# Modulation vectors of a two-block model: the products on VectorE, ScalarE and GpSimd, the sum over partitions on TensorE

## The chip, the core and the metric

One core of one Trainium2 chip. The metric is the device time of one execution, in microseconds (us). The engines are TensorE (PE; its weight loads are shown as PEld), VectorE (DVE), ScalarE (ACT), GpSimd (POOL) and SyncE (SP), whose queue issues the loads and stores here.

## The reference

Two blocks work on 512 tokens of width 1024, all in float32. The first has four layers (gated linear attention, GLA; a spatial gating unit, SGU; forgetting attention, FOX; GLA again). The second has two layers, runs on the tokens and on 256 context tokens, and each of its layers also has a feed-forward part (FFN). Every layer begins with a norm whose result is scaled and shifted, and ends with a gated addition to the residual. The shift, scale and gate are the modulation vectors, and only they matter here:

```python
cond = jax.nn.silu(c)
for i in range(DEPTH):
    mod = (cond @ w_mod[i] + b_mod[i])[:, None, :]
    shift, scale, gate = jnp.split(mod, 3, axis=-1)
    h = rms_norm(x, norm_pre_g[i]) * (1.0 + scale) + shift
    ...
    x = x + gate * rms_norm(o, norm_post_g[i])
```

In the first block each layer has 3 vectors of 1024 and one condition. In the second each layer has 6, and two conditions (one for the tokens, one for the context), so that two rows come out of one pass over the weights. A vector is a row of 1024 numbers times a 1024 x 1024 matrix: 4 MB of weights are read for each, and each weight is used once or twice.

## The kernel before

**Projections.** Every large product is done with operands split in two parts: a weight tile of 256 KB ([128, 512] elements) is loaded by SP into a ring of raw buffers (tag `wr`, 5 of them), ACT copies its leading part (line 256, into a ring `wh` of 4) and POOL or DVE subtracts that from the raw tile (line 257, into `wl`, 4 of them). PE then multiplies leading by leading, leading by rest and rest by leading (lines 307 to 309 and 351 to 353). PSUM results are evicted by ACT and DVE. The context stream of the second block has rings of its own (`cwr`, `cwh`, `cwl`).

**Modulation vectors.** The first layer's shift and scale are computed in `setup`, before all else, and are not touched. The other 22 vectors (10 with one condition, 12 with two) come from the generator `mods` (lines 373 to 393). For a vector it takes one PSUM bank, and for each of 8 chunks of 128 rows of the weights it loads [128, 1024] (512 KB, line 382) into one of `WM` = 2 buffers `wm`. One step later it issues four matmuls (line 386): the stationary operand is the condition's chunk, padded to 32 columns, the moving operand 256 columns of the weights, and the four results lie on the four groups of 32 partitions. After 8 chunks DVE evicts the bank (line 390), and SP stores one row per condition in DRAM (line 392). Later `mod_cols` (lines 425 to 438) or `gate_row` reads it back, adds the bias and makes columns or a broadcast row of it. The norm uses the columns on line 502. Line 585 is a gated addition to the residual, line 523 a scaling of a tile in the norm and line 524 the same on ACT.

**Order of the work.** The main stream is a generator, and `drain` takes steps of background queues after each of its steps: 0.6 steps of queue "m" (the vectors, in the order in which they are needed, then a position bias), and a rate by stage of queue "c" (the context stream). Where a vector is needed and not yet put out, `need` puts out all that is left up to it at once:

```python
def step(self, q, n=1):
    self.owed[q] += n
    while self.owed[q] >= 1:
        self.owed[q] -= 1
        if self.bg[q]:
            old, self.sk = self.sk, q
            try:
                next(self.bg[q][0][1])
            except StopIteration:
                self.bg[q].pop(0)
            self.sk = old
```

A vector takes 10 yields of `mods`. The order in which instructions are put out is their priority; a scheduler that simulates the engines' times (`schedule_with_timeline_sim=True`) then fixes the order on each engine and on SP's queue, and on the chip each engine runs its instructions in that order.

## Time and profile before

| | us |
|---|---|
| median of 3 runs | 3319.11 |
| the runs | 3316.0, 3319.11, 3320.16 |
| the profiled execution: span from its first to its last instruction | 3315.4 |

The profile is of one execution. It gives no other time of that execution than its span; the median of the runs lies 3.7 us above it. Line numbers (L386) are those of the kernel before; tiles are named after the stage that made them (`mods.wm` is the buffer `wm` of the stage `mods`; `pa` and `pp` are PSUM banks). "Busy" is the time in which an engine had an instruction running; for PE the ends of overlapping matmuls are modelled. An arrow `<-` after a time names what ended an idle time. A float32 matmul of line 386 appears as two records.

### The profile page before, as it was taken

Reading aid. Unit: us, or ns where it says so; the run is one execution under the profiler, and the core shown is the slowest. Engines: PE = TensorE matmul, PEld = TensorE weight load, DVE = VectorE, ACT = ScalarE, POOL = GpSimd, SP = SyncE. Lnnn points to the kernel's source line nnn. Section 1 sums busy time; section 2 is a strip of 40 time slices with the busy share of each in tenths; the row PEclk is TensorE's granted clock in tenths of the full one; section 3 lists DMA queues with packets and bytes.
Section 4 is the critical chain, followed back from the end, with each engine's and each line's share of the span. In section 5 each row is a group of like instructions: output and inputs, shape, how many; then the busy total and the mean of one; then the engine's idle time right before and its main releaser. Section 6 shows DMA issues by size and latency. Waiting matters only on the chain.

```text
span 3315.4 us, 63038 instructions
## 1 busy us (share of the span) xinstructions
PE 3154.1 (95%) x24399; PEld 2704.3 (82%) x24399; DVE 1699.2 (51%) x3578; ACT 1451.7 (44%) x3189; POOL 1307.3 (39%) x1320
## 2 busy tenths in 40 slices
PE   7999999899999999988989999899999989999999
PEld 4878889778778778887877899889889956789898
DVE  3744564454555555657888667531215476541112
ACT  3434544455444533345545544543325246543323
POOL 2544453322222344443642123554446510154445
PEclk9999999999999999998999999899999979999999
DMA  7355645754436524444753344433333310043332
GB/s 239 87 159 185 194 144 164 234 173 125 147 111 198 162 81 132 153 117 126 188 172 110 86 131 114 155 115 94 117 101 124 102 39 1 25 142 94 98 119 89
DMA packets 487155, 426.36 MB, mean 129 GB/s; under 512 B 108038, under 2 KB 441065, under 8 KB 486857
## 3 DMA queue, kind: packets, MB, share of 16 engines
q1 hardware_dynamic: 486857, 422.35, 42.5%
q8 instruction: 192, 3.15, 0.4%
q14 instruction: 106, 0.87, 0.1%
HBM read 383.66 MB, written 38.03 MB: 127 GB/s over the span
## 4 chain that ended last, share of the span: by engine, by line
PE 75%; DVE 11%; DMA 5%; ACT 4%; issue 3%; POOL 2%; SPq 1%; POOLq 0%; DVEq 0%; ACTq 0%
PE ffn.pp L352 6%; PE ffn.pp L351 6%; PE ffn.pp L353 5%; PE ffn.pp L308 3%; PE ffn.pp L307 3%; PE ffn.pp L309 3%; PE mods.pa L386 3%; PE out.pp L307 2%; PE out.pp L309 2%; PE out.pp L308 2%; DMA mods.wm<-in_w_mod_dram 2%; PE odda.pa L889 1%; PE fox.pp L308 1%; PE fox.pp L309 1%; PE fox.pp L307 1%
## 5 line engine op out<-in xcount | busy, mean ns | idle before, releaser
L257 POOL TENSOR_TENSOR ffn.wl<-ffn.wr,ffn.wh 128x512 fp32r<-128x512 f32 x258 | 333.5, 1294 | 355.0 <-ACT ffn.wh L256 355.0
L256 ACT ACTIVATE ffn.wh<-ffn.wr 128x512 fp32r<-128x512 f32 x258 | 162.5, 631 | 354.9 <-PE ffn.pp L353 144.3
L351 PE MATMUL ffn.pp<-pre.t,ffn.wh 128*128 128x512 f32 x672 | 261.5, 389 | 0.0
L352 PE MATMUL ffn.pp<-pre.t,ffn.wl 128*128 128x512 f32 x672 | 261.5, 389 | 0.0
L353 PE MATMUL ffn.pp<-pre.t,ffn.wh 128*128 128x512 f32 x672 | 261.4, 389 | 0.0
L308 PE MATMUL ffn.pp<-ffn.wl,ffn.t 128*128 128x256 f32 x656 | 185.3, 283 | 0.0
L309 PE MATMUL ffn.pp<-ffn.wh,ffn.t 128*128 128x256 f32 x656 | 184.9, 283 | 0.0
L307 PE MATMUL ffn.pp<-ffn.wh,ffn.t 128*128 128x256 f32 x656 | 184.7, 283 | 0.0
L591 DVE SCALAR_TENSOR_TENSOR ffn.t<-ffn.t,ffn.pp 128x512 f32<-128x512 f32 (+1 forms) x66 | 39.4, 596 | 252.2 <-ACT ffn.t L590 252.1
L257 POOL TENSOR_TENSOR gla.wl<-gla.wr,gla.wh 128x512 fp32r<-128x512 f32 x66 | 87.2, 1321 | 163.7 <-ACT gla.wh L256 158.5
L307 PE MATMUL gla.pp<-gla.wh,pre.t 128*128 128x256 f32 x512 | 149.4, 292 | 0.7 <-ACT gla.t L644 0.4
L308 PE MATMUL gla.pp<-gla.wl,pre.t 128*128 128x256 f32 x512 | 148.8, 291 | 0.0
L309 PE MATMUL gla.pp<-gla.wh,pre.t 128*128 128x256 f32 x512 | 148.4, 291 | 0.0
L353 PEld LDWEIGHTS ffn.pp<-pre.t,ffn.wh 128*128 128x128 f32 x672 | 126.2, 188 | 26.2
L351 PEld LDWEIGHTS ffn.pp<-pre.t,ffn.wh 128*128 128x128 f32 x672 | 126.2, 188 | 26.1
L352 PEld LDWEIGHTS ffn.pp<-pre.t,ffn.wl 128*128 128x128 f32 x672 | 126.2, 188 | 25.8
L257 POOL TENSOR_TENSOR ffn.cwl<-ffn.cwr,ffn.cwh 128x512 fp32r<-128x512 f32 x44 | 60.3, 1370 | 212.4 <-ACT ffn.cwh L256 183.9
L386 PE MATMUL mods.pa<-mods.wm,cond_c 128*32 128x256 f32 x1408 | 121.4, 398 | 16.8 <-DMA mods.wm<-in_w_mod_dram 16.7
L1133 DVE SCALAR_TENSOR_TENSOR ffn.t<-ffn.t,ffn.pp 128x512 f32<-128x512 f32 (+1 forms) x66 | 39.4, 597 | 176.3 <-PE ffn.pp L353 175.7
L256 ACT ACTIVATE ffn.cwh<-ffn.cwr 128x512 fp32r<-128x512 f32 x132 | 82.9, 632 | 102.8 <-PE ffn.pp L353 43.0
L308 PEld LDWEIGHTS ffn.pp<-ffn.wl,ffn.t 128*128 128x128 f32 x656 | 125.9, 192 | 0.2
L307 PEld LDWEIGHTS ffn.pp<-ffn.wh,ffn.t 128*128 128x128 f32 x656 | 125.6, 192 | 0.2
(786 smaller groups left out, 10843.8 us busy)
## 6 DMA issues: line engine op xcount, KB each, us to landing
mods.wm<-in_w_mod_dram SPq DMA_DIRECT2D x176, 512.0 KB
gla.wr<-in_gla_w_in_dram SPq DMA_DIRECT2D x96, 256.0 KB
ffn.wr<-in_w_ffn_gate_dram SPq DMA_DIRECT2D x88, 256.0 KB
ffn.wr<-in_w_ffn_up_dram SPq DMA_DIRECT2D x88, 256.0 KB
ffn.wr<-in_w_ffn_down_dram SPq DMA_DIRECT2D x88, 256.0 KB
fox.wr<-in_fox_w_in_dram SPq DMA_DIRECT2D x64, 256.0 KB
sgu.wr<-in_sgu_w_in_dram SPq DMA_DIRECT2D x48, 256.0 KB
out.res_x<-out.t SPq DMA_DIRECT2D x24, 512.0 KB
```

Source lines behind the costliest of these rows:

```text
L256: nc.scalar.activation(hi, src, AF.Copy)
L257: (lo_eng or nc.vector).tensor_tensor(lo, src, hi.bitcast(F32), op=ALU.subtract)
L307: nc.tensor.matmul(o, H.hi(kk, s), w[0][:, k], start=(kk == 0 and first), stop=False)
L308: nc.tensor.matmul(o, H.hi(kk, s), w[1][:, k], start=False, stop=False)
L309: nc.tensor.matmul(o, H.lo(kk, s), w[0][:, k], start=False, stop=(kk == K - 1 and last))
L351: nc.tensor.matmul(o, wh[:, k], H.hi(kk), start=(kk == 0), stop=False)
L352: nc.tensor.matmul(o, wl[:, k], H.hi(kk), start=False, stop=False)
L353: nc.tensor.matmul(o, wh[:, k], H.lo(kk), start=False, stop=(kk == K - 1))
L386: nc.tensor.matmul(ps[g * 32:(g + 1) * 32, :256], pad[:, j, :], ws[j][:, g * 256:(g + 1) * 256], start=(j == 0), stop=(j == 7))
L591: nc.vector.scalar_tensor_tensor(dst, dst, 1.0, z, ALU.add, ALU.mult)
L889: nc.tensor.transpose(pz[:, j:j + 128], P[:, j0 + j:j0 + j + 128], self.ident)
L1133: nc.vector.scalar_tensor_tensor(f, sg, 0.5, o[1], ALU.mult, ALU.mult)
```

## The change

`mods` works on half vectors of 512 columns. For each half it loads 8 tiles [128, 512] of 256 KB, again with 2 buffers. DVE multiplies the first tile by the first condition, one number per partition, and for the other seven multiplies and adds onto an accumulator. With two conditions, ACT multiplies each tile by the second condition and POOL adds the product onto a second accumulator; there is one buffer for the product. After the 8 chunks PE adds the accumulator's partitions: four matmuls of 128 columns per condition, with a stationary operand of 32 columns of which one is ones and the others zeros. DVE evicts [128, 128], and SP stores 512 columns per condition. Two chunks go into one step; a vector takes 9 yields. The constant `unit` is made in `setup` by three memsets on POOL. The raw weight ring `wr` has 4 buffers and not 5. All comments and docstrings are gone as well.

```diff
@@ setup
         nc.gpsimd.memset(self.zero, 0.0)
+        self.unit = self.const([128, 2, 32], "unit")
+        nc.gpsimd.memset(self.unit, 0.0)
+        for i in range(2):
+            nc.gpsimd.memset(self.unit[:, i, i:i + 1], 1.0)
@@ mods
         pad = self.cond[cname]
-        ps = self.psA()
-        ws = []
-        for k in range(8 + WM - 1):
-            if k < 8:
-                ws.append(self.wp.tile([128, D], F32, name=self.nm("wm"), tag="wm", bufs=WM))
-                nc.sync.dma_start(ws[k], W[k * 128:(k + 1) * 128, v * D:(v + 1) * D])
-            j = k - WM + 1
-            if j >= 0:
+        for c0 in range(v * D, (v + 1) * D, 512):
+            ws = []
+            accs = [self.wp.tile([128, 512], F32, name=self.nm("wacc"), tag=f"wacc{i}", bufs=1) for i in range(ncond)]
+            for k in range(8 + WM - 1):
+                if k < 8:
+                    ws.append(self.wp.tile([128, 512], F32, name=self.nm("wm"), tag="wm", bufs=WM))
+                    nc.sync.dma_start(ws[k], W[k * 128:(k + 1) * 128, c0:c0 + 512])
+                j = k - WM + 1
+                if j >= 0:
+                    c = [pad[:, j, i:i + 1] for i in range(ncond)]
+                    if j == 0:
+                        nc.vector.tensor_scalar(accs[0], ws[j], c[0], None, ALU.mult)
+                    else:
+                        nc.vector.scalar_tensor_tensor(accs[0], ws[j], c[0], accs[0], ALU.mult, ALU.add)
+                    if ncond == 2:
+                        p = self.wp.tile([128, 512], F32, name=self.nm("wprod"), tag="wprod", bufs=1) if j else accs[1]
+                        nc.scalar.activation(p, ws[j], AF.Copy, scale=c[1])
+                        if j:
+                            nc.gpsimd.tensor_tensor(accs[1], accs[1], p, op=ALU.add)
+                if k % 2:
+                    yield
+            ps = self.psA()
+            for i, acc in enumerate(accs):
                 for g in range(4):
-                    nc.tensor.matmul(ps[g * 32:(g + 1) * 32, :256], pad[:, j, :], ws[j][:, g * 256:(g + 1) * 256],
-                                     start=(j == 0), stop=(j == 7))
-            yield
-        sb = self.t("t1", [128, 256])
-        nc.vector.tensor_copy(sb, ps[:, :256])
-        for i in range(ncond):
-            nc.sync.dma_start(scr[i, v * D:(v + 1) * D].rearrange("(g n) -> g n", n=256), sb[i:128:32, :])
+                    nc.tensor.matmul(ps[g * 32:(g + 1) * 32, :128], self.unit[:, i, :], acc[:, g * 128:(g + 1) * 128],
+                                     start=(i == 0), stop=(i == ncond - 1))
+            sb = self.t("t1", [128, 128])
+            nc.vector.tensor_copy(sb, ps[:, :128])
+            for i in range(ncond):
+                nc.sync.dma_start(scr[i, c0:c0 + 512].rearrange("(g n) -> g n", n=128), sb[i:128:32, :])
         yield
@@ constants
-NBUF = {..., 'wr': 5, ...}
+NBUF = {..., 'wr': 4, ...}
```

## Rows read from the trace of the kernel before

**Rows 1.** The page: span, and busy time, share and instructions of each engine.
```profile
span 3315.4 us, 63038 instructions
...
PE 3154.1 (95%) x24399; PEld 2704.3 (82%) x24399; DVE 1699.2 (51%) x3578; ACT 1451.7 (44%) x3189; POOL 1307.3 (39%) x1320
```

**Rows 2.** The page: the chain that ended last, share of the span by engine.
```profile
PE 75%; DVE 11%; DMA 5%; ACT 4%; issue 3%; POOL 2%; SPq 1%; POOLq 0%; DVEq 0%; ACTq 0%
```

**Rows 3.** Windows: length, busy us per engine (instructions), clock, DMA share, GB/s.
```profile
58.00:300.00 242.00, 233.93 (x1679) 195.18 (x1678) 132.80 (x221) 92.31 (x169) 110.54 (x116) 0.99 0.42 129
300.00:1110.00 810.00, 775.71 (x6383) 657.84 (x6382) 428.00 (x927) 389.89 (x879) 264.84 (x262) 0.98 0.56 172
1110.00:1420.00 310.00, 295.62 (x2718) 249.01 (x2717) 179.71 (x363) 123.12 (x261) 130.37 (x158) 0.98 0.43 129
1420.00:3315.00 1895.00, 1812.23 (x13381) 1580.43 (x13379) 940.43 (x2018) 825.11 (x1829) 783.52 (x749) 0.97 0.36 106
```

**Rows 4.** The tile mods.wm: its instructions, what they waited for, who waited.
```profile
L386 PE MATMUL mods.pa<-mods.wm,cond_c x1408: 379/379/637, 58.9 to 1397.0; 128*32 128x256 f32 x176
L382 SPq DMA_DIRECT2D mods.wm<-in_w_mod_dram x176: 327/340/1179, 22.9 to 1391.9; - x176
...
  DMA mods.wm<-in_w_mod_dram: 40.7, 40
...
  PE mods.pa L386: 16.7, 19
```

**Rows 5.** The chain of 58 to 1420 us by line, shares of it.
```profile
by line: PE mods.pa L386 6.2%; DMA mods.wm<-in_w_mod_dram 4.3%; issue 3.4%; PE out.pp L307 3.2%; PE fox.pp L308 3.0%; PE fox.pp L309 3.0%; PE out.pp L308 3.0%; PE fox.pp L307 3.0%; PE out.pp L309 3.0%; PE sgu.pp L307 2.9%; PE sgu.pp L308 2.
```

**Rows 6.** Timeline from 588 us: start, length, engine, line, operation.
```profile
589.06 0.28 PE L351 MATMUL gdnp.pp<-pre.t,gdnp.cwh 128*128 128x256 f32 x1
...
589.27 0.59 PEld L386 LDWEIGHTS mods.pa<-mods.wm,cond_c 128*32 128x32 f32 x16
589.27 1.07 PE L386 MATMUL mods.pa<-mods.wm,cond_c 128*32 128x256 f32 x16
...
590.27 0.39 PE L352 MATMUL gdnp.pp<-pre.t,gdnp.cwl 128*128 128x256 f32 x1
```

**Rows 7.** The windows of rows 3 up to 1420, line 386 alone: sum.
```profile
sum 1362.00, PE 121.39 PEld 31.36; mean PE 40.47 PEld 10.45
```

**Rows 8.** DVE by shape, 58 to 1420 us: busy us, mean ns.
```profile
L257 DVE TENSOR_TENSOR gla.wl<-gla.wr,gla.wh 128x512 fp32r<-128x512 f32 x30 | 27.8, 926 | 37.1 <-ACT gla.wh L256 35.6 <-DMA gdng.t<-gdn_tok_ctx 1.4
...
L585 DVE SCALAR_TENSOR_TENSOR out.t<-out.t,out.rr,out.t 128x512 f32<-128x512 f32 x24 | 19.5, 853 | 2.6 <-POOL out.rr L532 2.4
...
L523 DVE TENSOR_SCALAR pre.t<-out.t,pre.rr 128x512 f32<-128x512 f32 x12 | 6.8, 566 | 6.5 <-POOL pre.rr L532 6.5
...
L257 DVE TENSOR_TENSOR mlap.cwl<-mlap.cwr,mlap.cwh 128x512 fp32r<-128x512 f32 x4 | 2.8, 692 | 10.9 <-ACT mlap.cwh L256 10.9
```

**Rows 9.** ACT by shape, 58 to 1420 us: product by a column.
```profile
L524 ACT ACTIVATE pre.t<-out.t,pre.rr 128x512 f32<-128x512 f32 x12 | 8.6, 719 | 6.5 <-POOL pre.rr L532 6.5
```

**Rows 10.** POOL by line, 58 to 1420 us: two operands, 128x512.
```profile
L257 POOL TENSOR_TENSOR gla.wl<-gla.wr,gla.wh 128x512 fp32r<-128x512 f32 x62 | 82.3, 1328 | 148.4 <-ACT gla.wh L256 145.3 <-issue 2.9
```

**Rows 11.** Waits of SP queue, 58 to 1420: us, times, longest.
```profile
SPq L382 <- PE mods.pa L386: 204.6, 118, 15.1
...
SPq L382 <- DMA mods.wm<-in_w_mod_dram: 41.0, 35, 4.7
```

**Rows 12.** The tile gla.wl: its DVE instructions, ns min/median/max.
```profile
L257 DVE TENSOR_TENSOR gla.wl<-gla.wr,gla.wh x32: 281/693/2737, 43.2 to 1311.8; 128x512 fp32r<-128x512 f32 x31, 128x128 fp32r<-128x128 f32 x1
```

**Rows 13.** The page, costliest groups: weight splits on ACT.
```profile
L256 ACT ACTIVATE ffn.wh<-ffn.wr 128x512 fp32r<-128x512 f32 x258 | 162.5, 631 | 354.9 <-PE ffn.pp L353 144.3
```

**Rows 14.** SP timeline, 588 to 622 us: a vector stored.
```profile
621.57 0.55 SPq L392 DMA_DIRECT2D mod_a<-mods.t  x1
```

**Rows 15.** DVE timeline, 618 to 654 us: its columns ready, used.
```profile
628.81 0.15 DVE L437 SCALAR_TENSOR_TENSOR out.mcol<-out.pa,cols 128x8 f32<-128x8 f32 x1
...
652.66 1.45 DVE L502 TENSOR_SCALAR pre.t<-pre.pa,out.mcol 128x256 f32<-128x256 f32 x3
```

More of the change, by code (lines that the diff above doesn't have):

```diff
@@ L2193, in first_block @@
         self.H = H
-NBUF = {'at': 4, 'sq': 1, 't4': 28, 'wr': 5, 'wh': 4, 'wl': 4, 'cwr': 3, 'cwh': 2, 'cwl': 2, 't2': 10, 't1': 5}
+NBUF = {'at': 4, 'sq': 1, 't4': 28, 'wr': 4, 'wh': 4, 'wl': 4, 'cwr': 3, 'cwh': 2, 'cwl': 2, 't2': 10, 't1': 5}
 WM, WSZ = 2, 512
```

## The prediction

> **What bounds the kernel now.** I read the busy times first. TensorE (PE) is busy 95% of a span of 3315.4 us, VectorE (DVE) 51%, ScalarE (ACT) 44%, GpSimd (POOL) 39% [rows 1]. The median of the three runs shown, 3319.1 us, is 3.7 us above that span; the sum is made against the span, and 3.7 us are added at the end. A difference of 0.2%, 6.6 us, is about what a measurement of this kernel can tell from no change.
>
> Busy is not the same as deciding, so next comes the chain of waits: PE carries 75% of it, DVE 11%, DMA 5%, ACT 4%, POOL 2% [rows 2]. A microsecond taken from PE is thus likely to count, and one added to DVE is likely to be covered.
>
> Then where the changed work runs. The matmuls of the modulation vectors (line 386) start at 58.9 us and the last starts at 1397.0 us [rows 4]; the stretch 58 to 1420 us, 1362 us long, holds all of it. There PE is busy 233.9 + 775.7 + 295.6 = 1305 us (96%), DVE 132.8 + 428.0 + 179.7 = 740.5 us (54%), ACT 605 us (44%), POOL 506 us (37%) [rows 3]. After 1420 us nothing of the change runs except the smaller ring of raw weights. In the chain of this stretch alone, line 386 is the largest single entry with 6.2%, 84 us, and the loads of its operand come second with 4.3%, 59 us [rows 5].
>
> **The change part by part.** There are 22 vectors: 10 with one condition, 12 with two. Before, each takes 8 loads of 512 KB and 8 groups of 4 matmuls over 256 columns, in the trace as 8 records each: 176 groups.
>
> *Removed from PE.* A busy time of overlapping matmuls is no price, so I take a place in the timeline: two groups (16 records) begin at 589.27 us and the next matmul of another line begins at 590.27 us [rows 6], 0.50 us a group. 176 x 0.50 = 88 us; the chain's 84 us agrees and is the lower bound, the busy time of 121 us [rows 7] contains modelled ends of matmuls that overlap. The Trainium skill says the same of such rows (Perfetto Trace Analysis, Identifying the Most-Contended Engine: matmul occupancy is no good measure, because matmuls are pipelined); by busy time the sum would come out 33 us lower than mine. PE also stood 16.7 us waiting for these loads, 19 times [rows 4]; it no longer waits for them. Bounds 0 and the chain's 59 us. I take 17, what PE itself lost.
>
> *Added to PE.* The partitions are added per half vector and condition: 10 x 2 + 12 x 2 x 2 = 68 groups of 8 records over 128 columns. With half the columns, proportion gives 0.25 us; the 16 weight loads of two groups took 0.59 us [rows 6], so 0.30 us a group where they set the pace. I take 0.30: 20 us. Bounds 17 and 34 (no cheaper than before). A new wait stands in PE's order, for the finished sum, 44 times. Before, a group waited 0.095 us on average (16.7/176); the sum passes more engines, so I take twice that, 8 us. Bounds 0 and 44 x 0.88 = 39 us (0.88 us is the mean of the 19 waits). Behind it in PE's order stand the projections' matmuls.
>
> *Added to DVE.* 44 products (tensor_scalar, nearest row 0.566 us) and 308 multiply-adds of 128x512 with all operands in SBUF (nearest row line 585, the same operation, 0.853 us) [rows 8]: 25 + 263 = 288 us. DVE rises from 54% to 75% of the stretch. An added operation matters only where work of the chain stands behind it on DVE. With DVE's 11% of the chain and half an operation of mean delay that is 288 x 0.11 / 2 = 16 us; bounds 0 and 32. The eviction of a vector (line 390) becomes two of half the size: nothing, it lies in DVE's idle time. DVE also takes over the wait for the load, and evictions and weight splits queue behind it. PE and its weight-load queue saw 40.7 us of such waits [rows 4]; twice as many loads make 81 us, and 11% of that is 9 us.
>
> *Added to ACT and POOL.* 12 x 2 x 8 = 192 products on ACT with a scale per partition (0.719 us [rows 9]), 138 us, and 12 x 2 x 7 = 168 adds on POOL (1.328 us [rows 10]), 223 us. By the same reckoning with 4% and 2%: 3 + 2 = 5 us, bounds 0 and 10. Each ACT product after the first waits until POOL has read the only product buffer; ACT's splits of weights stand behind it.
>
> *Loads and SP's queue.* 352 loads of 256 KB in the place of 176 of 512 KB, two in flight, so half the bytes ahead. SP issues one in 0.34 us [rows 4]: 60 us more on SP, and 34 more stores of some 0.5 us [rows 14], 17 us. SP already stands 204.6 + 41.0 us before these loads, waiting for their two buffers [rows 11], with weight loads queued behind; now DVE and ACT free the buffers. I put this at nothing, because ACT's weight split itself waits for PE to free a slot: the weights are there first [rows 13]. If that cover goes, the first rival below is the result.
>
> *One raw weight buffer less* (4 in the place of 5): nothing, by the same row. Upper bound: DMA's 5% of the chain is 166 us, less the 59 of the removed loads; a fifth of the rest is 21 us. The three small memsets at the start run under the first loads.
>
> Sum: -88 - 17 + 20 + 8 + 16 + 9 + 5 = **-47 us**. 3315.4 - 47 + 3.7 = **3272 us**.
>
> **Rivals.** *DVE stands before the loads, and PE runs dry (slower).* Before, a step issued one load and used the one of a step earlier. Now a step issues two and uses one of them at once: 22 x 2 x 4 = 176 operations on DVE ask for a load issued just before. If each holds DVE for the 0.88 us that a wait took, that is 155 us; with half reaching PE, 77 us, the 77 us that PE gains net (88 + 17 - 20 - 8) are gone, and the 21 us for the other engines remain: 3340 us. It decides from 0.44 us a load reaching PE. For it: the vectors of a layer's head come shortly before the norm that uses them; one is stored at 621.57 us, its columns are ready at 628.81 us and used at 652.66 us [rows 14, 15], only 24 us of slack. Against it: 1362 - 740 - 288 = 334 us of idle DVE, and weights that are ahead. Chance 0.12.
>
> *DVE and POOL hold each other up, and the gain is eaten.* The same subtraction takes 0.692 us on average in one stage and 0.926 us in the GLA projections [rows 8], with a longest case of 2.737 us [rows 12]. That is what two engines on one port would look like. With 0.926 us for the new operations (22 us more) and 0.234 us for a foreign DVE operation at each of the 168 adds (39 us), DVE gets 349 us. If a fifth of it reaches the end, 70 us in the place of my 16 + 9, the time is 3317 us: no change. Against it: even then DVE is at 80% of the stretch, under PE. The Trainium skill has this as a rule that speaks against the change (GPSIMD Engine Reference, Specifications: GpSimd's SBUF interfaces are shared with VectorE, with contention from VectorE instructions with two SBUF inputs, which the multiply-add is). By that rule, the trace agrees in kind; chance 0.10.
>
> *All of the chain's share goes.* If the loads' 59 us go and not 17, the sum is -84 - 59 + 20 + 30 = -93 us: 3226 us. For it: the chain of the stretch. Against it: a chain names one path, and the next is usually close. Chance 0.18.
>
> *It does nothing.* The matmuls may only have filled gaps that the slow chains of the GLA layer leave on PE; then the 88 us turn into idle time: about 3319 us. Against it: line 386 on the chain. Chance 0.05.
>
> **How the numbers follow.** The forecast, 3272 us, has 0.55. Faster by over 0.2%: 0.55 + 0.18 + 0.02 of the second rival = 0.75. Within 0.2%: 0.05 of the second and 0.03 of the last = 0.08. Slower: 0.12 + 0.03 + 0.02 = 0.17. The range goes from 3215 us, just under the third rival, to 3330 us, past "no change" with the 21 us of the buffer bound largely spent. Some 0.07 lie below and 0.10 above.
>
> **What would show it.** Right: 544 matmul records on the new line, under 30 us; PE busy in 58 to 1420 us (and what takes its place) down by some 70 us; DVE near 1030 us and still under PE in that stretch; the time after 1420 us unchanged within a few us. Wrong: PE idle time in that stretch grown by over 50 us with DVE or wl as the releaser (first rival), multiply-adds of over 0.93 us (second), or waits for raw weights after 1420 us (the buffer).

## The result and the profile after

The changed kernel takes 3479.9 us (median of 4 runs, 3471.6 to 3486.2) where the kernel before took 3319.1 us beside it (4 runs, 3316.0 to 3320.2): slower by a ratio of 1.049, 95% interval 1.0465 to 1.0514, that is by 161 us. The forecast was 3272 us, faster, and its range ended at 3330. One run of the experiments is left out below, the first of the edit e9: it took 3685.7 us at a granted clock of 0.78 in its last 1895 us, where the two kernels' profiles and every other profile here show 0.96 to 0.98.

The page of the changed kernel: its span, the busy time of each engine, and the three groups that took over the products (L396 the multiply-add, L400 the ScalarE product, L402 the GpSimd addition).

```profile
span 3475.0 us, 62851 instructions
...
PE 3141.8 (90%) x23535; PEld 2744.6 (79%) x23535; DVE 2057.1 (59%) x3952; ACT 1567.1 (45%) x3380; POOL 1587.5 (46%) x1491
...
L396 DVE SCALAR_TENSOR_TENSOR mods.wacc<-mods.wm,cond_c,mods.wacc 128x512 f32<-128x512 f32 x308 | 304.4, 988 | 137.2 <-DMA mods.wm<-in_w_mod_dram 135.3
...
L402 POOL TENSOR_TENSOR mods.wacc<-mods.wacc,mods.wprod 128x512 f32<-128x512 f32 x168 | 242.9, 1446 | 159.9 <-ACT mods.wprod L400 121.4
...
L400 ACT ACTIVATE mods.wprod<-mods.wm,cond_c 128x512 f32<-128x512 f32 x168 | 121.1, 721 | 157.9 <-DMA mods.wm<-in_w_mod_dram 81.1
```

The span grew by 159.6 us against [rows 1] and TensorE's busy time shrank by only 12.3. DVE got 358 us more, ACT 115, POOL 280. The multiply-add takes 988 ns on average, where I had 853; the addition 1446, where I had 1328; the product 721 against 719.

Where the time went is told by the windows, cut 1895 us before the end as in [rows 3]; the vectors' last matmul starts at 1492.6 us. These are the columns of [rows 3]: length, busy us of PE, PEld, DVE, ACT and POOL, granted clock, DMA share, GB/s.

```profile
58.00:300.00 242.00, 219.17 (x1427) 193.68 (x1426) 182.54 (x284) 96.19 (x177) 126.88 (x120) 0.93 0.41 120
300.00:1110.00 810.00, 673.01 (x5139) 602.17 (x5140) 582.34 (x1020) 402.44 (x851) 388.00 (x318) 0.89 0.50 151
1110.00:1580.00 470.00, 402.14 (x3420) 349.82 (x3417) 335.56 (x595) 224.86 (x480) 272.72 (x268) 0.91 0.43 126
1580.00:3475.00 1895.00, 1812.64 (x13330) 1578.65 (x13328) 934.86 (x2006) 823.52 (x1825) 781.91 (x748) 0.97 0.36 105
```

The last 1895 us stand beside the last 1895 us of before [rows 3]: PE busy 1812.64 us and 1812.23 us, the same. So nearly all of the loss lies in the stretch of the vectors, 58 to 1580 us in the place of 58 to 1420 us (a later projection, `oddq`, starts its first matmul at 2757.5 us and 2606.5 us before, so 151 of the 160 us are lost by then). PE is busy 1294 us in the stretch (1305 before) and idle 228 us (57 before), and its granted clock is 0.89 to 0.93 where it was 0.98 to 0.99.

The same stretch in one piece, first whole, then the vectors' new matmul line (L408) alone:

```profile
58.00:1580.00 1522.00, 1294.31 (x9980) 1145.67 (x9979) 1100.44 (x1898) 723.50 (x1507) 787.61 (x705) 0.90 0.47 138
58.00:1580.00 1522.00, 30.27 (x544) 12.67 (x544) 0.90 0.47 138
```

The vectors' own matmuls fell from 121.39 us [rows 7] to 30.27, but PE as a whole is busy only 11 us less. By the difference all other matmuls of the stretch are busy 80 us longer. Of that, 67 more of their records in the stretch make some 9 us; the other 70 us are slower matmuls, at a granted clock of 0.90 in the place of 0.98. So the loss has two parts, 171 us more idle time on PE and 80 us of longer busy time, against 91 us that the vectors' line gave back.

What PE waits for is the third view. First its longest waits in 58 to 1580 us of the changed kernel (us, times, longest), then two lines of the kernel before, 58 to 1420 us.

```profile
PE pre.pa L515 <- DVE pre.t L544: 53.1, 7, 12.1
PE fox.pa L1068 <- DVE fox.t L966: 16.1, 6, 4.2
PE glah.pa L744 <- POOL glah.t L737: 11.2, 16, 2.5
PE glah.pa L744 <- DVE glah.t L738: 9.9, 10, 1.7
PE fox.pa L910 <- ACT fox.at L885: 9.7, 5, 3.6
...
PE mods.pa L408 <- POOL mods.wacc L402: 7.4, 4, 2.6
```

```profile
PE glah.pa L723 <- POOL glah.t L716: 8.9, 16, 1.2
...
PE pre.pa L494 <- DVE pre.t L523: 0.8, 2, 0.4
```

The largest wait is for `pre.t` of the norm at a layer's head: 53.1 us, where the same wait took 0.8 us before. The others are chains of small DVE, ACT and POOL operations in GLA and FOX, a few microseconds each. PE's wait for the vectors' own sums is small, 7.4 us for the one from POOL. No single wait makes 171 us of new idle time; many late results of other work add up to it.

Last, the tile `mods.wm` and SP's queue, which answer to [rows 4] and [rows 11].

```profile
L389 SPq DMA_DIRECT2D mods.wm<-in_w_mod_dram x352: 322/335/1751, 22.9 to 1479.7; - x176
L396 DVE SCALAR_TENSOR_TENSOR mods.wacc<-mods.wm,cond_c,mods.wacc x308: 716/752/2904, 34.4 to 1485.0; 128x512 f32<-128x512 f32 x154
...
  DVE mods.wacc L396: 135.3, 117
  ACT mods.wprod L400: 81.1, 34
```

```profile
SPq L389 <- DVE mods.wacc L396: 207.1, 177, 4.1
...
SPq L389 <- ACT mods.wprod L400: 66.8, 58, 4.0
SPq L389 <- DMA mods.wm<-in_w_mod_dram: 55.6, 60, 2.9
```

DVE stands 135.3 us in 117 waits before its loads, and SP 330 us for the two buffers (246 us before). That looks like the first rival. The experiments speak against it.

One seam shows the pattern: the head of the second layer, 352 to 381 us. The windows (columns as above) and the PE timeline of the changed kernel (start, length, engine, line, operation, idle before and its releaser):

```profile
352.00:370.00 18.00, 5.26 (x30) 3.42 (x30) 13.86 (x24) 7.46 (x21) 10.73 (x14) 0.50 0.44 135
370.00:381.00 11.00, 7.20 (x31) 6.53 (x32) 9.89 (x18) 7.06 (x17) 8.03 (x12) 0.50 0.58 200
```

```profile
361.68 0.65 PE L408 MATMUL mods.pa<-mods.wacc,unit 128*32 128x128 f32 x8 [2.47 <-POOL mods.wacc L402]
370.60 1.94 PE L515 MATMUL pre.pa<-ident,pre.t 128*128 128x128 f32 x8 [8.27 <-DVE pre.t L544]
...
378.84 0.41 PE L312 MATMUL sgu.pp<-sgu.wh,pre.t 128*128 128x256 f32 x1
379.05 0.41 PE L313 MATMUL sgu.pp<-sgu.wl,pre.t 128*128 128x256 f32 x1
...
381.28 0.28 PE L313 MATMUL sgu.pp<-sgu.wl,pre.t 128*128 128x256 f32 x1
381.39 0.28 PE L314 MATMUL sgu.pp<-sgu.wh,pre.t 128*128 128x256 f32 x1
```

DVE's timeline in the same stretch:

```profile
346.36 2.42 DVE L606 SCALAR_TENSOR_TENSOR out.t<-out.t,out.rr,out.t 128x512 f32<-128x512 f32 x2
348.70 2.41 DVE L396 SCALAR_TENSOR_TENSOR mods.wacc<-mods.wm,cond_c,mods.wacc 128x512 f32<-128x512 f32 x2
351.85 1.48 DVE L544 TENSOR_SCALAR pre.t<-out.t,pre.rr 128x512 f32<-128x512 f32 x1 [0.73 <-POOL pre.rr L553]
...
360.87 1.03 DVE L394 TENSOR_SCALAR mods.wacc<-mods.wm,cond_c 128x512 f32<-128x512 f32 x1 [1.07 <-DMA mods.wm<-in_w_mod_dram]
363.02 0.75 DVE L396 SCALAR_TENSOR_TENSOR mods.wacc<-mods.wm,cond_c,mods.wacc 128x512 f32<-128x512 f32 x1 [1.11 <-DMA mods.wm<-in_w_mod_dram]
...
369.96 0.48 DVE L544 TENSOR_SCALAR pre.t<-out.t,pre.rr 128x512 f32<-128x512 f32 x1 [0.47 <-POOL pre.rr L553]
```

PE is busy 5.26 of 18 us, and one idle time of 8.27 us ends when DVE delivers `pre.t`. Meanwhile DVE works through residual additions (L606), the norm's scaling (L544, which makes `pre.t`) and the vectors' multiply-adds by turns; it stands 1.07 us before a load at 360.87 and 1.11 us at 363.02, and single operations are stretched: L544 takes 1.48 us at 351.85, where POOL has an addition of the vectors running (from 351.78 us, 1.27 us long), and 0.48 us at 369.96, where POOL has only operations of one column. The granted clock of the stretch is 0.50, the lower of the two levels (in the kernel before it is 1.00 from 320 to 360 us, where the same layer begins): the matmuls of 128x256 start 0.21 us apart up to 379.05 us, and 0.11 us apart at 381.28.

### The profile page after: what moved, and what is told of

Same layout as the page of the kernel before. It is cut to its first block, busy times and chain, and to the rows that moved or that the text cites. A ratio compares the mean times of both kernels' runs of the same rounds, so it can differ in the third digit from the quotient of the medians.

```text
span 3475.0 us, 62851 instructions
## 1 busy us (share of the span) xinstructions
PE 3141.8 (90%) x23535; PEld 2744.6 (79%) x23535; DVE 2057.1 (59%) x3952; ACT 1567.1 (45%) x3380; POOL 1587.5 (46%) x1491
## 5 line engine op out<-in xcount | busy, mean ns | idle before, releaser
L262 POOL TENSOR_TENSOR ffn.wl<-ffn.wr,ffn.wh 128x512 fp32r<-128x512 f32 x258 | 333.6, 1294 | 356.5 <-ACT ffn.wh L261 355.7
L396 DVE SCALAR_TENSOR_TENSOR mods.wacc<-mods.wm,cond_c,mods.wacc 128x512 f32<-128x512 f32 x308 | 304.4, 988 | 137.2 <-DMA mods.wm<-in_w_mod_dram 135.3
L402 POOL TENSOR_TENSOR mods.wacc<-mods.wacc,mods.wprod 128x512 f32<-128x512 f32 x168 | 242.9, 1446 | 159.9 <-ACT mods.wprod L400 121.4
L400 ACT ACTIVATE mods.wprod<-mods.wm,cond_c 128x512 f32<-128x512 f32 x168 | 121.1, 721 | 157.9 <-DMA mods.wm<-in_w_mod_dram 81.1
L314 PE MATMUL gla.pp<-gla.wh,pre.t 128*128 128x256 f32 x512 | 153.2, 300 | 3.3 <-DVE pre.t L262 3.3
L312 PE MATMUL gla.pp<-gla.wh,pre.t 128*128 128x256 f32 x512 | 153.5, 300 | 2.8 <-ACT gla.t L665 2.4
```

Of the source, the lines that this page charges most:

```text
L262: (lo_eng or nc.vector).tensor_tensor(lo, src, hi.bitcast(F32), op=ALU.subtract)
L312: nc.tensor.matmul(o, H.hi(kk, s), w[0][:, k], start=(kk == 0 and first), stop=False)
L314: nc.tensor.matmul(o, H.lo(kk, s), w[0][:, k], start=False, stop=(kk == K - 1 and last))
L396: nc.vector.scalar_tensor_tensor(accs[0], ws[j], c[0], accs[0], ALU.mult, ALU.add)
L400: nc.scalar.activation(p, ws[j], AF.Copy, scale=c[1])
L402: nc.gpsimd.tensor_tensor(accs[1], accs[1], p, op=ALU.add)
```

## The experiments

Three explanations are told apart here. **Loads:** DVE, ACT and SP stand before the loads of the vectors (the first rival). **Work:** the operations added to DVE, ACT and POOL delay other work in their order, whatever they wait for. **Shape:** half tiles, with half the bytes ahead, cost by themselves. Times stand against the kernel before in the same round (3318 to 3323 us) or against the changed kernel's 3480 us, whose four runs lie 15 us apart.

**e1: the multiply-adds on 16 columns.**

```diff
-nc.vector.scalar_tensor_tensor(accs[0], ws[j], c[0], accs[0], ALU.mult, ALU.add)
+nc.vector.scalar_tensor_tensor(accs[0][:, :16], ws[j][:, :16], c[0], accs[0][:, :16], ALU.mult, ALU.add)
```

> The changed kernel, but the 308 multiply-adds on VectorE take 16 of the 512 columns (the first vector of each pair of conditions is therefore left out of the computation but for 16 columns of each half). Every wait for a load stays, the work goes. Theory 'waits' (VectorE stands in order before the half loads, 135 us of waiting in the changed kernel): hardly better, 3430 to 3480 us. Theory 'work' (the 304 us of multiply-adds delay what stands behind them on VectorE): most of the 160 us comes back, 3300 to 3360 us.

3428.5 us (one run), 51 less than the changed kernel. DVE's waits for the loads did not go but rose to 211.5 us (135.3 before). DVE's work counts, and its standing there costs less than it looks. The cut operations still take 133 us on DVE, so 172 us of work were taken away.

**e2: the multiply-adds read no load.** Their work stays; the sum is not that of the weights.

```diff
-nc.vector.scalar_tensor_tensor(accs[0], ws[j], c[0], accs[0], ALU.mult, ALU.add)
+nc.vector.scalar_tensor_tensor(accs[0], accs[0], c[0], accs[0], ALU.mult, ALU.add)
```

> The changed kernel, but the multiply-adds read the accumulator twice and not the loaded tile (the first condition's vectors are left out of the computation). The work stays at 512 columns, VectorE no longer waits for loads, and SP's loads no longer wait for VectorE. Theory 'waits': most of the 160 us comes back, 3300 to 3370 us. Theory 'work': 3420 to 3480 us.

3484.0 us (one run): 4 us above the changed kernel. The multiply-adds themselves got 19 us longer in total (1051 ns each), so the 135.3 us that DVE stood before loads can be worth some 15 us at most. ACT still stands 81.8 us before its loads here, so the run says nothing of ACT's waits.

**e3: the second condition left out.** No products on ACT, no additions on POOL; the context's rows are not computed.

```diff
-            accs = [self.wp.tile([128, 512], F32, name=self.nm("wacc"), tag=f"wacc{i}", bufs=1) for i in range(ncond)]
+            accs = [self.wp.tile([128, 512], F32, name=self.nm("wacc"), tag=f"wacc{0}", bufs=1)] * ncond
...
-                    if ncond == 2:
+                    if False:
```

> The changed kernel with the second condition left out: no products on ScalarE, no adds on GpSimd, 24 multiplies and 168 products and adds fewer, the first condition's sum is stored in both rows. VectorE does all that it did. Theory 'second condition' (GpSimd's adds hold VectorE up and ScalarE waits for the one product buffer): most of the 160 us comes back, under 3360 us. Theories 'waits' and 'work' of VectorE alone: 3400 to 3470 us.

3383.4 us (one run): 96 of the 161 us come back. DVE waits for the loads as it did (133.5 us), and its multiply-adds take 870 ns in the place of 988.

**e4 to e6, e8 and e15: the shape of the loads.** e4 is the kernel before with TensorE's products on the half tiles and steps of the changed kernel:

```diff
+for c0 in range(v * D, (v + 1) * D, 512):
...
-                ws.append(self.wp.tile([128, D], F32, name=self.nm("wm"), tag="wm", bufs=WM))
+                    ws.append(self.wp.tile([128, 512], F32, name=self.nm("wm"), tag="wm", bufs=WM))
...
-                    nc.tensor.matmul(ps[g * 32:(g + 1) * 32, :256], pad[:, j, :], ws[j][:, g * 256:(g + 1) * 256],
+                        nc.tensor.matmul(ps[g * 32:(g + 1) * 32, :128], pad[:, j, :], ws[j][:, g * 128:(g + 1) * 128],
...
+                if k % 2:
+                    yield
```

> The kernel before, products still on TensorE, but on half tiles of 256 KB with two buffers and two loads a step as in the changed kernel (5 raw weight buffers as before). Theory 'smaller loads' (half the bytes ahead, twice the issues, SP's queue blocked): a good part of the 160 us appears here too, 3380 us or more. Theories 'waits' or 'work' on VectorE: within 20 us of before plus some 30 us for the doubled number of matmuls, 3310 to 3360 us.

3404.6 us (one run), 83 more than the kernel before. PE waits 36.7 us for the loads in the place of 16.7, and SP stands 406 us before them. e5 is e4 with four half tiles in flight, so as many bytes ahead as before:

```diff
-WM, WSZ = 2, 512
+WM, WSZ = 4, 512
```

> The kernel before on half tiles of 256 KB, two loads a step, but with four buffers and a use three loads later: the same bytes in flight as before. Theory 'too little in flight' (two half buffers make each load wait for the one before the last, SP's queue stands there, and weights and residual loads behind it come late): most of the 83 us that the half tiles cost with two buffers comes back, 3310 to 3345 us. Theory 'twice the loads and matmuls' (number of issues, fixed cost of small matmuls): stays at 3380 us or more.

3373.4 us, ratio 1.0159 (1.0129 to 1.0189) to the kernel before: 53 us more, outside the 3310 to 3345 that I gave to bytes in flight as the whole cause. Some 30 of the 83 come back. (With four buffers a vector takes 11 steps and not 9, so e5 and e6 also spread the vectors over more of the order.) e15 is e4 with a `yield` after every load and 1.14 steps in the place of 0.6:

```diff
-                if k % 2:
-                    yield
+                yield
...
-MRATE, MB = 0.6, 2
+MRATE, MB = 1.14, 2
```

> The kernel before on half tiles, two buffers, but one load in each step as before and 1.14 steps in the place of 0.6, so that the vectors keep their pace. Two loads in one step: the loss falls from 83 to under 40 us, 3360 us or less. Half tiles themselves (half the bytes ahead, 17 us more matmul): 3385 us or more.

3412.4 us, ratio 1.0273 (1.0242 to 1.0303): as slow as e4. Two loads in one step are not what costs; the half tiles are, in part through the bytes ahead (e5). e8 is the kernel before with every 512 KB load issued as two of 256 KB into the same buffer:

```diff
-nc.sync.dma_start(ws[k], W[k * 128:(k + 1) * 128, v * D:(v + 1) * D])
+for h in range(2):
+    nc.sync.dma_start(ws[k][:, h * 512:(h + 1) * 512], W[k * 128:(k + 1) * 128, v * D + h * 512:v * D + (h + 1) * 512])
```

> The kernel before with each 512 KB load of the vectors' weights issued as two of 256 KB into the two halves of the same buffer. Theory 'too little in flight': within 15 us of before, since as many bytes are ahead. Theory 'twice the loads': 3350 us or more.

3334.4 us (one run; before 3311.3 to 3330.3 in seven): 11 us over the median of before and 4 us over its longest run, so the 176 extra issues cost little, and one run can't tell how little. e6 gives the changed kernel four half tiles in flight, paid for with raw buffers:

```diff
-NBUF = {..., 'wr': 4, ...}
-WM, WSZ = 2, 512
+NBUF = {..., 'wr': 2, ...}
+WM, WSZ = 4, 512
```

> The changed kernel with four buffers of 256 KB and a use three loads later; the room comes from the raw weight ring, 2 in the place of 4. Theory 'too little in flight': 3400 to 3440 us (40 to 80 us better than the changed kernel's 3480), if the two raw buffers cost nothing; the stretch after the vectors, where only the raw ring differs, shows their price by itself. Theory 'work on VectorE and GpSimd': within 25 us of 3480 us in the stretch of the vectors.

3500.0 us (one run), 20 more than the changed kernel, though DVE's waits for the loads fell from 135.3 us to 31.3 and ACT's from 81.1 to 11.5. Two raw buffers fewer are in that number, and their price is not known (one fewer cost 13 us, e13 below), so it says no more than this: with the waits nearly gone nothing was gained that two raw buffers don't eat up. Together with e2 it leaves little room for the theory of the loads where DVE is concerned; for ACT it rests on e6 alone.

**e9: all added operations on 16 columns** (the first product of a half vector keeps its 512). It is the shape of the changed kernel without most of its work.

```diff
... (the multiply-adds as in e1)
-nc.scalar.activation(p, ws[j], AF.Copy, scale=c[1])
+nc.scalar.activation(*((p[:, :16], ws[j][:, :16]) if j else (p, ws[j])), AF.Copy, scale=c[1])
...
-nc.gpsimd.tensor_tensor(accs[1], accs[1], p, op=ALU.add)
+nc.gpsimd.tensor_tensor(accs[1][:, :16], accs[1][:, :16], p[:, :16], op=ALU.add)
```

> The changed kernel with the multiply-adds, the products (all but the first of a half vector) and the additions cut to 16 columns; loads, waits, steps and matmuls as they are. The sums are left out but for 16 columns. Work in the engines' order (my theory): almost all of the loss goes, 3290 to 3370 us, and the norm's matmuls wait less than 30 us for pre.t. The loads' pattern (two half tiles in a step, one used at once, the rival): the loss stays for the most part, 3400 us or more.

3358.6 us (two runs), ratio 1.0122 (1.0069 to 1.0176) to the kernel before. 121 of the 161 us go with the work, though DVE's wait for the loads rises to 214 us. But PE still waits 51.6 us for `pre.t` over the whole span, more than the 30 I had said, and 41 us of loss remain: the shape, the smaller ring and what PE gives up are together no gain. The cut operations still take time (106 us the multiply-adds, 51 the products, 51 the additions), so not all of the 41 is the shape. In the stretch of the vectors alone the wait for `pre.t` is still this:

```profile
PE pre.pa L515 <- DVE pre.t L544: 32.2, 10, 5.2
```

So more than half of the longest wait of the list, 53.1 us, stays without most of the added work.

**e13, e10, e14, e16, e11: the work alone, beside TensorE's products.** These leave the kernel before as it is, with its 512 KB loads, and put the changed kernel's operations beside the matmuls; nobody reads what they compute. All have 4 raw buffers, to make room, so e13, which is that alone, is their zero. They ran in two rounds, so the differences are taken between the ratios; each of them is good to some 10 us either way.

```diff
-NBUF = {..., 'wr': 5, ...}
+NBUF = {..., 'wr': 4, ...}
```

> The kernel before with 4 raw weight buffers in the place of 5, nothing else. If the buffer costs nothing, as the last 1895 us of the two kernels say: 3310 to 3330 us. If the runs that add work to the kernel before owe part of their loss to it: 3335 us or more, and that much is to be taken off each of them.

3335.2 us (10 runs), ratio 1.0040 (1.0024 to 1.0056): 13 us, and not nothing. e10 adds DVE's work:

```diff
+acc = self.wp.tile([128, 512], F32, name=self.nm("wacc"), tag="wacc0", bufs=1)
...
+for h in range(2):
+    wj = ws[j][:, h * 512:(h + 1) * 512]
+    if j == 0 and h == 0:
+        nc.vector.tensor_scalar(acc, wj, pad[:, j, 0:1], None, ALU.mult)
+    else:
+        nc.vector.scalar_tensor_tensor(acc, wj, pad[:, j, 0:1], acc, ALU.mult, ALU.add)
```

> The kernel before (raw ring 4), with the changed kernel's work on VectorE put beside TensorE's: one product and 15 multiply-adds of 128x512 for each vector, on the two halves of each 512 KB tile; nobody reads their sum. TensorE's work, the loads' size and their steps stay as before. Work in the order: about the 51 us that cutting these operations took off the changed kernel, 3350 to 3400 us, with PE's wait for pre.t up from 18.7 to 35 us or more. Loads' pattern: within 10 us of the kernel before.

3404.8 us, ratio 1.0251 (1.0217 to 1.0285). Less e13's 0.40% that is 2.1%, 70 us. PE's wait for `pre.t` did not rise as I had said (20.9 us over the span, 18.7 before). That wait in the vectors' stretch, DVE's new group there, and the window that answers to [rows 3] (the profiled run, 3386.0 us, is the shortest of the four):

```profile
PE pre.pa L501 <- DVE pre.t L530: 2.6, 3, 1.0
```

```profile
L394 DVE SCALAR_TENSOR_TENSOR mods.wacc<-mods.wm,cond_c,mods.wacc 128x512 f32<-128x512 f32 x327 | 280.7, 858 | 154.0 <-DMA mods.wm<-in_w_mod_dram 150.5
```

```profile
58.00:1489.00 1431.00, 1337.57 (x10724) 1120.40 (x10723) 999.06 (x1847) 601.58 (x1301) 539.32 (x534) 0.96 0.48 145
```

PE has the same work, 10724 matmuls against the 1679 + 6383 + 2718 of [rows 3], and is idle 93 us in the place of 57 and busy 1338 us in the place of 1305, at a clock of 0.96 in the place of 0.98. Half of the loss of that run is idle time in small pieces, half is slower matmuls. e14 is e10 without the reads of the weights:

```diff
-nc.vector.scalar_tensor_tensor(acc, wj, pad[:, j, 0:1], acc, ALU.mult, ALU.add)
+nc.vector.scalar_tensor_tensor(acc, acc, pad[:, j, 0:1], acc, ALU.mult, ALU.add)
```

> As the kernel before with VectorE's added work, but the 330 multiply-adds read their own sum twice and no weights; only the first operation of a vector reads a tile. Their time on VectorE stays, its wait for the loads (150.5 us, 75 times) and its share in setting the buffers free go. The work itself: 3380 to 3410 us, as with the waits. The waits: 3340 us or less.

3416.0 us, ratio 1.0275 (1.0244 to 1.0307), 78 us over e13. The waits for the loads make none of e10's loss: it is the operations. e16 adds only the second condition's products on ACT:

```diff
+for h in range(2 if ncond == 2 else 0):
+    p = self.wp.tile([128, 512], F32, name=self.nm("wprod"), tag="wprod", bufs=1)
+    nc.scalar.activation(p, ws[j][:, h * 512:(h + 1) * 512], AF.Copy, scale=pad[:, j, 1:2])
```

> The kernel before (raw ring 4) with the 192 products of 128x512 on ScalarE alone, without GpSimd's additions; nobody reads them. If GpSimd's additions make the loss (VectorE stretched beside them, ScalarE held by the product buffer): within 25 us of e13. If ScalarE's own 138 us make it: 3370 us or more.

3362.6 us, ratio 1.0117 (1.0083 to 1.0151): 0.77% or 26 us over e13, for 192 products of 0.72 us. ACT also stands 93.8 us before the loads in this run, and no run here takes that away from it by itself, so the 26 us are the products and their waits together:

```profile
L390 ACT ACTIVATE mods.wprod<-mods.wm,cond_c 128x512 f32<-128x512 f32 x192 | 138.0, 719 | 94.9 <-DMA mods.wm<-in_w_mod_dram 93.8
```

e11 adds POOL's additions too:

```diff
     nc.scalar.activation(p, ws[j][:, h * 512:(h + 1) * 512], AF.Copy, scale=pad[:, j, 1:2])
+    if j:
+        nc.gpsimd.tensor_tensor(p, p, p, op=ALU.add)
```

> The kernel before (raw ring 4), with the second condition's work put beside TensorE's: for each vector with two conditions 16 products on ScalarE and 14 additions on GpSimd, 128x512 each, through one buffer; nobody reads them. Work in the order: towards the 96 us that leaving the second condition out took off the changed kernel, 3370 to 3430 us. If VectorE's work alone counts: within 15 us of the kernel before.

3388.4 us, ratio 1.0217 (1.0195 to 1.0238), another 1.0% or 33 us for the additions and for ACT's wait for the one product buffer (47.0 us):

```profile
L392 POOL TENSOR_TENSOR mods.wprod<-mods.wprod 128x512 f32<-128x512 f32 x168 | 183.0, 1090 | 152.0 <-ACT mods.wprod L390 141.5
L390 ACT ACTIVATE mods.wprod<-mods.wm,cond_c 128x512 f32<-128x512 f32 x192 | 138.1, 719 | 92.5 <-POOL mods.wprod L392 47.0
```

The additions take 1090 ns here, where they read one buffer twice, and 1446 ns in the changed kernel, so e11 has 183 us of the 243 us of POOL's work. One line tells what POOL does to DVE: the gated addition to the residual (line 585 of the kernel before, 853 ns there [rows 8]), in e16 and then in e11, by shape, 58 us to the vectors' end:

```profile
L588 DVE SCALAR_TENSOR_TENSOR out.t<-out.t,out.rr,out.t 128x512 f32<-128x512 f32 x24 | 19.9, 869 | 4.4 <-POOL out.rr L535 4.2
```

```profile
L590 DVE SCALAR_TENSOR_TENSOR out.t<-out.t,out.rr,out.t 128x512 f32<-128x512 f32 x24 | 27.6, 1190 | 3.1 <-POOL out.rr L537 1.6 <-DMA gla.wr<-in_gla_w_in_dram 1.2
```

The same 24 operations take 869 ns beside ACT's products and 1190 ns when POOL's additions run too. By the Trainium skill (SBUF — State Buffer, on the port pair that DVE and GpSimd share) a DVE instruction with two SBUF inputs contends with a GpSimd instruction that reads SBUF; the trace agrees, 321 ns an operation here. It is not the whole picture: the norm's scaling (L523 of the kernel before), which has one tensor as input, rises too, from 581 to 780 ns, and DVE's subtractions of weights, which have two, by 65 ns at most.

**e12: a mixture.** DVE's method for the ten vectors with one condition, out of 512 KB loads that hold two row chunks of a half vector; TensorE's for the other twelve.

```diff
+if ncond == 1:
+    yield from self.mods1(scr, cname, W, v)
+    return
...
+ws.append(self.wp.tile([128, 2, 512], F32, name=self.nm("wm"), tag="wm", bufs=WM))
+nc.sync.dma_start(ws[k], W[k * 256:(k + 1) * 256, c0:c0 + 512].rearrange("(a p) n -> p a n", p=128))
...
```

> The ten vectors with one condition by VectorE's multiply-adds, out of 512 KB loads that hold two row chunks of a half vector, one load in a step as before; the twelve with two conditions by TensorE as before. Raw ring 4. TensorE loses 80 groups of 0.50 us and gets 20 of 0.30 us, 34 us less. Work in the order: VectorE's 140 us cost at the rate of 51 for 288 some 25 us: 3310 us, within 20 either way. If only the pattern of the loads cost time: 3285 us.

3349.5 us, ratio 1.0090 (1.0068 to 1.0112): 17 us over e13's level by the ratios, outside what I gave it. So 140 us of DVE work and the changed loads cost more than 34 us less on TensorE gave. That raised the next question.

**e17 and e18: TensorE's work taken away, nothing added.** Parts of the columns are left out of the sums. In e17 seven of a vector's eight chunks have one matmul in the place of four:

```diff
-for g in range(4):
+for g in range(4 if j == 0 else 1):
...
-                                     start=(j == 0), stop=(j == 7))
+                                     start=(j == 0), stop=(j == (0 if g else 7)))
```

> The kernel before with 11 of the 32 matmuls of a vector: the first chunk has all four, the other seven only one each (their other three quarters of the columns are left out of the sums). Loads, waits, buffers, steps as before; nothing is added. 21/32 of 88 us, 58 us, go if a matmul taken from TensorE counts in full as the prediction had it: 3262 us (3250 to 3275). If half of it only turns into idle time on TensorE: 3290 us. If all of it: 3320 us.

e17 took 3345.0 us, ratio 1.0079 (1.0052 to 1.0106), and its expectation was built on a wrong price. PE's timeline, one group of four matmuls (8 records) in the kernel before and one group of one (2 records) in e17:

```profile
618.07 0.64 PE L386 MATMUL mods.pa<-mods.wm,cond_c 128*32 128x256 f32 x8
618.64 0.38 PE L308 MATMUL out.pp<-out.wl,sgu.t 128*128 128x256 f32 x1
```

```profile
621.64 0.62 PE L386 MATMUL mods.pa<-mods.wm,cond_c 128*32 128x256 f32 x2
622.19 0.38 PE L309 MATMUL out.pp<-out.wh,sgu.t 128*128 128x256 f32 x1
```

0.57 us for four, 0.55 us for one: the four go to four groups of 32 columns of the array and run side by side, as the Trainium skill describes it (TensorE: Matmul & The Clock Gate, Packing small matmuls). e17 thus took next to nothing from PE (the line is busy 112 us in the place of 121). That it still lost 26 us says what an edit of this kernel can cost in itself; like e13's, it may put all instructions after it in another order. The 26 us of e16, the 33 of e11 and the 17 of e12, each taken by itself, are of that size; the 70 and 78 of DVE's operations and the 59 of e11 over e13 are well above it.

e18 is e17 with the one matmul of the middle six chunks cut to 16 columns, which does take time from PE:

```diff
... (the loop over g and the stop flag as in e17)
-nc.tensor.matmul(ps[g * 32:(g + 1) * 32, :256], pad[:, j, :], ws[j][:, g * 256:(g + 1) * 256],
+n = 256 if j in (0, 7) else 16
+nc.tensor.matmul(ps[g * 32:(g + 1) * 32, :n], pad[:, j, :], ws[j][:, g * 256:g * 256 + n],
```

> The kernel before, where of a vector's eight chunks the middle six have one matmul of 16 columns each in the place of four of 256 (the rest is left out of the sums), the first has all four and the last one of 256. Loads, waits, buffers and steps as before; nothing is added. Six of eight groups, 132, fall from 0.50 us to about 0.15: 46 us less on TensorE. If that counts in full: 3274 us, or some 3295 with the 15 to 26 us that small edits of this kernel have cost (e8, e13, e17). If it turns into idle time: 3320 to 3345 us.

PE's timeline in e18, two groups:

```profile
320.96 0.30 PE L387 MATMUL mods.pa<-mods.wm,cond_c 128*32 128x16 f32 x4
321.19 0.39 PE L307 MATMUL out.pp<-out.at,gla.t 128*128 128x256 f32 x1
```

0.23 us, so 0.115 us a group in the place of 0.50. The windows of e18 up to the vectors' end and after it, then the first of them for the vectors' line alone (sum):

```profile
58.00:1420.00 1362.00, 1271.64 (x9867) 1116.63 (x9865) 740.20 (x1512) 606.17 (x1310) 509.03 (x536) 0.95 0.51 154
1420.00:3315.00 1895.00, 1804.80 (x13372) 1574.53 (x13370) 937.15 (x2018) 823.91 (x1828) 787.14 (x749) 0.97 0.37 106
```

```profile
sum 1362.00, PE 60.43 PEld 25.91; mean PE 60.43 PEld 25.91
```

The line's own busy time fell from 121.39 us [rows 7] to 60.43. PE as a whole is busy 33.6 us less in the stretch than before [rows 3]: by the difference the other matmuls got 27 us longer, at a clock of 0.95 in the place of 0.98, and the rest became idle time, 90 us in the place of 57. The time is 3325.0 us (12 runs), ratio 1.0011 (0.9995 to 1.0026): nothing gained over the kernel before. But e17 is the same edit with PE's time left in, and over e17 the gain is 0.68% or some 23 us of the 57 us (132 groups from 0.55 to 0.115 us) that were taken. So between none and two fifths of a microsecond taken from PE reached the end, by which of the two is the zero; in full it did not count by either.

## Why the prediction was wrong

**Point by point,** by the terms of the sum. Shares are in us of 3320; e2 and e4 are single runs:

| term | predicted | measured | by |
|---|---|---|---|
| matmuls taken from PE, with their waits | -88 - 17 | for 132 of 176 groups: 0, or -23 | e18 against before, or against e17 |
| the other matmuls of the stretch | 0, not named | some +70 us of busy time, clock 0.90 for 0.98 | changed kernel |
| one group of 128 columns on PE | 0.30 us | 0.29 us (two from 673.20 to 673.78 us) | changed kernel |
| DVE's operations | +16 | +70, +78 | e10, e14 less e13 |
| DVE's waits for the loads | +9 | nothing | e2, e14 |
| ACT's products | +3 | +26, with ACT's waits for loads | e16 less e13 |
| POOL's additions | +2 | +33, with ACT's waits for the buffer | e11 less e16 |
| loads and SP's queue | 0 | with PE as the consumer +83; the shape with little work +41, buffer included | e4; e9 |
| one raw buffer less | 0, bound 21 | +13 | e13 |

The shape with little work (41) and the three kinds of work (70 + 26 + 33) make 170 us, where 161 were measured. That is near, but no proof that the parts are complete: e9 still has part of the work in its 41, each part is good to 10 us or so, and taken away from the changed kernel the work is worth 51 us (e1) and 96 (e3) in two parts, but 121 at once (e9).

**The step that failed first** is the cover of the added operations: "an added operation matters only where work of the chain stands behind it on DVE", priced by an engine's share of the chain times half an operation. DVE's operations reach the end with a quarter of their time (70 of some 290 us), ACT's and POOL's with a fifth (26 of 138; 33 of 183); I had 6, 2 and 1%. An engine's share of the chain tells what a given order waits for. In the changed kernel PE's new waits lie in the norms, in GLA and in FOX, where DVE, ACT, POOL and PE take turns on small tiles: idle time of 46% on DVE was not idle time at those places, where DVE was the engine that PE waited for (53.1 + 16.1 + 9.9 us in the list above). That the added operations alone make these waits is not shown: of the 53.1 us for `pre.t`, 32.2 stay when the work is cut to 16 columns (e9), and DVE's work beside the old matmuls makes 2.6 (e10).

The sum also has no term for what idle time does to the clock. It took PE's other matmuls to stay as long as they were, and they got some 70 us longer (0.90 in the place of 0.98).

**The second** is the -88 us. "A microsecond taken from PE is thus likely to count" was read from PE's 75% of the chain. The price of a group was right in the timeline, and taking it away for 132 groups left the end where it was: the time became idle time and slower matmuls. That is the fourth rival, to which I gave 0.05. What e18 can't tell is whether a gain of 13 to 26 us is hidden under what small edits cost here; against e17 it is 23.

**The cover of the loads**, put at nothing, is the third. The row that I took for it [rows 13] is of the FFN, whose first split runs at 2126.5 us, after the last vector; it says nothing of the stretch where the loads changed. There half tiles cost 83 us with PE as the consumer (e4).

**The first rival** had the sign and not the mechanism. DVE does stand before the loads, 135.3 us, as it said. But without those waits nothing is gained (e2, e14), nor with four loads in flight and two raw buffers fewer (e6). The signature that I had written down for it, PE idle time grown by over 50 us with DVE as the releaser, came true, and would have misled: the releaser is DVE for the norm's `pre.t` and not for the sums. **The second rival** had a mechanism that is there: multiply-adds at 988 ns, over the 0.93 us that I had set as its sign, against 870 ns in e3 and 858 in e10 without POOL's additions; and L590 above. Its 70 us for DVE is near what e10 and e14 measured, by a fifth of 349 us where the runs have a quarter of 290; what it had wrong is that it left PE's gain and the small prices of ACT, POOL and the loads in place. **The third rival** left the 8 us of PE's new wait out of its sum, which would be 3234 us with them.

**What held:** PE's matmuls on the new line are 544 records and busy 30.3 us, just over the 30 I had said; the product on ACT 0.721 us; the time after the vectors unchanged. **What didn't:** PE busy in the stretch fell by 11 us and not by 70, and DVE rose to 1100 us and not 1030, though still under PE. Of the raw buffer's 13 us, 7 lie in the vectors' stretch (their last matmul starts at 1404.2 us in e13 and at 1397.0 before), and not only after 1420 us, where I had looked for them.

**What stays open.** Which order of instructions makes the loss is not shown: the kernel's scheduler lays out every engine's order anew for each edit, and the waits that grew are many and small (in e10's stretch none but that for the vectors' own loads is over 9.0 us). Why half tiles cost 83 us where PE reads them is settled only in part: 30 us come back with as many bytes ahead (e5), some 17 are longer matmuls (by an estimate, 352 groups of 0.30 us against 176 of 0.50), the rest is not told apart. Nor is it told apart how much of ACT's 26 us is its waits for loads, and why most of the wait for `pre.t` stays in e9. None of the versions was faster than the kernel before.

## What to carry to other kernels

A high share of the busy time, or of the chain of waits, doesn't show that an engine's time counts in full, nor that its neighbours are covered: before work is moved from it to "idle" engines, take some of it away, and put the same work on the others with nobody reading it. Both are edits of a few lines, and here they would have shown beforehand that the gain is small and the cost is not. Look at the seams, where engines take turns, and not at a stage's mean; and run an edit that should cost nothing, to know what an edit costs.

## What the runs showed of the hardware

A group of one matmul with 32 stationary columns holds PE as long as four on four column groups (0.55 and 0.57 us). Beside GpSimd's additions of two operands, DVE's gated addition to the residual went from 869 to 1190 ns (e16, e11) and the multiply-adds of the changed kernel take 988 ns, 870 without the second condition's work (e3); the subtractions of weights, also with two operands, rose by 65 ns at most. And PE's idle time goes with a second price, slower matmuls: with 57 us of idle time in the stretch the clock was 0.98, with 90 us 0.95 and the other matmuls 27 us longer (e18), with 228 us 0.90 and some 70 us longer (the changed kernel). In the seam of 352 to 381 us, with PE busy 5.26 of 18 us at first, the granted clock was 0.50, the 1.2 GHz level, and with PE at work again from 370.60 us, with pauses, the matmuls at 379.05 us still started 0.21 us apart, those at 381.28 us 0.11.
